# First column piece of v from x times scale, and a new order of the first 140 microseconds

## The chip, the cores and the metric

The kernel runs on one core of one Trainium2 chip. The metric is the device time of that core in microseconds (us), the median of three runs. Five engines matter here: TensorE (PE) for products, VectorE (DVE), ScalarE (ACT), GpSimd (POOL) and SyncE (SP), whose queue issues most of the loads. "Weight load" (PEld) is PE's load of the stationary operand.

## The reference, cut to what matters

One step of a two-layer encoder over 1024 prompt rows and 32 sample rows, with D = 1024. Each layer is a mixer and a feed-forward part, each with an RMS norm before and after it and with a conditioning (shift, scale, gate) that comes from a condition vector.

```
mod = silu(c) @ w_ada[i] + b_ada[i]
sh1, sc1, gt1, sh2, sc2, gt2 = split(mod, 6)
h = rmsnorm(x, g_norm[i, 0]) * (1 + sc1) + sh1
# layer 0: spatial gating
z = gelu(h @ w_in)            # 1024 -> 4096
u, v = split(z, 2)            # 2048 each
v = rmsnorm(v, g_v)
mix = (u * (w_s v + b_s)) @ w_out
x = x + gt1 * rmsnorm(mix, g_norm[i, 1])
# then a feed-forward part of width 4096 with squared ReLU; layer 1 has a pooling mixer
```

With r the root of a row, h = r * x * scale + shift, where scale is g_norm * (1 + sc1) and belongs to a feature, r to a row. So h @ w is r * ((x * scale) @ w) + shift @ w.

## The kernel before

The rows are kept transposed, features on the 128 partitions, in three tiles (`TILES`, L27): two of 384 prompt rows and one of 256 prompt rows with the 32 sample rows. In blocks of 128 rows these are blocks 0 to 2, 3 to 5, and 6, 7 and 8 (the sample rows). Weights and the modulated rows are each split into a high and a low part ("wh", "wl"; "hh", "hl"), and a product is three matmuls: wh with hh, wl with hh, wh with hl. ACT makes wh by a copy (L422), DVE makes wl by a subtraction.

Before anything else stands the v half of the first product. It is made in four column pieces of 512; a piece p of a block b, here (p, b), is 24 matmuls of 128x512 (16 for block 8), into one PSUM place. `v_mm` (L910) issues them, `v_end` (L933) reads the place out: gelu, a square that accumulates, and a store.

To get there the kernel loads x blocks, turns them by TensorE transposes (`x_turn`; copies out by DVE at L586 or ACT at L588), sums squares on ACT (`x_squares`, L565), computes the roots (`spread`, L715: ACT's Sqrt, a reciprocal and a Newton step on DVE), spreads them over the partitions with a diagonal and a product with ones ("pb"), and `apply` (L853) makes mt = x * scale * r on DVE, hh = mt + shift on ACT, hl on DVE. `first_norm(t)` (L887) does this for tile t; its generators are called h0, h1 and h2.

The conditioning is a product with a matrix of 1024 x 6144. A slice is 256 of its columns, two loads of 512 KB. Slices 0 to 3 are the first shift, 4 to 7 the first scale; these are made on PE (`do_ada_pe`, L472: 16 small matmuls, a DVE transpose, a fold "adat"). All later slices are made on DVE (`do_ada`, L500: eight steps "aa" of 128x256 per load, then a transpose and a reduction per slice).

All loads stand in one list, `stream`, and `issue` (L395) issues them in that order on SP, as far as buffers are free: three raw places (`RAW_SLOTS`) for weights and slices that are dropped after use, and 16 places (`W_SLOTS`) for split weights and early raws.

The order around the change is set in two ways. From the first load up to the products of piece 0 a list of calls under `tc.manual_schedule` (L991 to L1047) fixes each engine's order. Everything behind it, including the slices 8 and up, is placed by a planner, which may put an instruction of later code between those of the fixed list. `early_mm` (L961) issues the products of piece 0 for blocks 0 to 4 pair by pair of k, as the modulated rows come; block 5 follows, then `v_order` (L1073): (1,0) to (1,5), then blocks 6 to 8 of pieces 0 and 1, then pieces 2 and 3.

Of the kernel before, what the change touches and what calls it, by code (L numbers as in the profile page):

```python
# [15 lines left out]
P = 128  # L16
# [18 lines left out]
def tile_stream_encoder_step(  # L35
# [144 lines left out]
    def load_vectors(i, part):  # L180
        at = sum(k for _, k in rows[i][: part.start])
        for ap, k in rows[i][part]:
            nc.scalar.dma_start(vec_rows[i][at : at + k, :P], ap)
            at += k
# [6 lines left out]
    def turn_conditions():  # L191
        raw = vec_rows[2]
        nc.vector.memset(csil32, 0.0)
        act(out=raw[0:16, P : 2 * P], in_=raw[0:16, :P], func=AF.Silu)

        act(out=raw[0:16, 2 * P : 2 * P + 1], in_=epsT[0:16, :], func=AF.Sqrt)
# [5 lines left out]
    def turn_vectors():  # L202
        for raw, v in zip(vec_rows, vecs):
            n = v.shape[1]
            pt = ps_ms("rowT")
            nc.tensor.transpose(pt[:, :n], raw[:n, :P], ident[:n, :n])
            nc.vector.tensor_copy(v, pt[:, :n])
# [131 lines left out]
    for b in range(3):  # L339
        add_x(b)  # L340
    for q in range(4):
        for j in (8 + 2 * q, 9 + 2 * q, 2 * q, 2 * q + 1):
            add_ada(0, j)
        add_w(*v_item(0, q))
        if q == 0:
            for b in range(3, 6):
                add_x(b)
# [30 lines left out]
    state = {"issued": 0, "next": 0, "raw": 0, "used": 0, "folds": 0}  # L378
    deferred = []

    def in_raw(k):
# [5 lines left out]
    x_rows = [  # L387
        room("h", t, f"x_rows{t}")
        .rearrange("p k n -> p (k n)")[:, : ncol[t] // P * D]
        .rearrange("p (b k n) -> p b k n", k=KB, n=P)  # L390
        for t in range(NT)
    ]
    junk = room("l", NT - 1, "xsq")

    def issue():  # L395
        while state["issued"] < len(stream):
            k = state["issued"]
            kind, key, ap, shape = stream[k]
            if in_raw(k):
                if state["raw"] == RAW_SLOTS:  # L400
                    return
                state["raw"] += 1
                r = t_raw(f"raw{k}")
            elif kind == "x":
                r = x_rows[key // 3][:, key % 3] if key < 8 else junk[:, :, P : 2 * P]
            else:
                r = work.tile([P, 1024], F32, tag="W", bufs=W_SLOTS, name=f"raw{k}")
            if kind == "x":
                nr = P if key < 8 else DEC
                i = (nc.scalar if key == 2 else nc.sync).dma_start(  # L410
                    r[:nr], ap.rearrange("t (k n) -> t k n", n=P)
                )
            else:
                i = nc.sync.dma_start(r.rearrange("p (a b) -> p a b", a=shape[0]), ap)
            raws[k] = r
            loads[key] = i.ins
            state["issued"] += 1

    def do_w(key, r):
        wh = work.tile([P, 1024], F32R, tag="W", bufs=W_SLOTS, name="wh_" + "_".join(map(str, key)))  # L420
        wl = work.tile([P, 1024], F32R, tag="W", bufs=W_SLOTS, name="wl_" + "_".join(map(str, key)))
        act(out=wh, in_=r, func=AF.Copy)  # L422
        witem[key] = (wh, wl)
        if key == ("v", 0, 0):
            late_lo.append(lambda: tt(out=wl, in0=r, in1=wh.bitcast(F32), op=ALU.subtract))
        else:
            tt(out=wl, in0=r, in1=wh.bitcast(F32), op=ALU.subtract)
# [135 lines left out]
    def x_squares(b, r):  # L563
# [8 lines left out]
    def x_turn(b, r):  # L572
# [3 lines left out]
        for half in range(2):  # L576
# [8 lines left out]
            if half == 0 or t == 0:  # L585
# [5 lines left out]
    x_turns = deque()  # L591

    def do_x(b, r):
        x_squares(b, r)
        if b < 3:
            x_turn(b, r)
        else:
            x_turns.append(lambda: x_turn(b, r))
# [10 lines left out]
    def stream_step():  # L609
# [18 lines left out]
        if in_raw(k):  # L628
# [85 lines left out]

    def spread(t, ss, tag, out, dg):  # L715
# [5 lines left out]
        ts(ms[:, :nb], ss[:, :nb], 1.0 / D, EPS, op0=ALU.mult, op1=ALU.add)  # L721
        act(out=r0[:, :nb], in_=ms[:, :nb], func=AF.Sqrt)
        nc.vector.reciprocal(out=r0[:, :nb], in_=r0[:, :nb])
        tt(out=q[:, :nb], in0=r0[:, :nb], in1=r0[:, :nb], op=ALU.mult)
        stt(out=q[:, :nb], in0=q[:, :nb], scalar=-0.5, in1=ms[:, :nb], op0=ALU.mult, op1=ALU.mult)
        stt(out=r0[:, :nb], in0=q[:, :nb], scalar=1.5, in1=r0[:, :nb], op0=ALU.add, op1=ALU.mult)
        yield False
        pb = ps_ms(f"pb_{tag}")
        for b, (c0, w) in enumerate(blk):
            act(out=dg[:w, c0 : c0 + w], in_=ident[:w, :w], func=AF.Copy, scale=r0[:w, b : b + 1])  # L730
        for b, (c0, w) in enumerate(blk):
            mm(pb[:, c0 : c0 + w], ones[:w, :], dg[:w, c0 : c0 + w], start=True, stop=True)
        out.append(pb)
# [119 lines left out]
    def apply(t, l, cf, sh, r, keep=False):  # L853
        hh[t] = room("h", t, f"hh{l}_{cf}_{t}", F32R)
        hl[t] = room("l", t, f"hl{l}_{cf}_{t}", F32R)
# [40 lines left out]

    def products(ps, n, terms):
# [8 lines left out]

    ssqv = small.tile([P, 9, 4], F32, name="ssqv")
# [25 lines left out]
    def v_end(ps, p, b):  # L933
        m = P if b < 8 else DEC
        vt = t_x(f"vt{p}_{b}", [P, 512])
        z = ps
        if b == 8:
# [21 lines left out]
    h0, h1, h2 = (first_norm(t) for t in range(NT))  # L959

    def early_mm(bs, q):  # L961

        wh, wl = witem[("v", 0, q)]
        for second in (False, True):
            for b in bs:
                t, c0 = b // 3, b % 3 * P
                tick(0.46 if second else 0.92)
                for k in range(2):
                    kb = 2 * q + k
                    a_h, a_l = hh[t][:, kb, c0 : c0 + P], hl[t][:, kb, c0 : c0 + P]  # L970
                    w = slice(k * 512, k * 512 + 512)
                    for a in (a_h,) if second else (a_h, a_l):
                        mm(
                            early_ps[b],
                            a,
                            (wl if second else wh)[:, w],
                            start=kb == 0 and a is a_h and not second,
                            stop=kb == KB - 1 and second,
                        )
# [5 lines left out]
    def conditions(q):  # L985

        stream_to("ada", (0, 4 + q, 1))
        stream_to("ada", (0, q, 1))
        pe_folds.pop(0)()

    with tc.manual_schedule():  # L991
        load_vectors(2, slice(0, 2))
        issue()
        load_vectors(2, slice(2, 4))
        load_vectors(0, slice(0, 1))
        load_vectors(1, slice(0, 1))
        turn_conditions()
        stream_to("x", 1)
        turn_vectors()
        stream_to("x", 2)  # L1000
        next(h0)
        conditions(0)
        statistics(h0)
        stream_to("w", ("v", 0, 0))
        pe_folds.pop(0)()
        for q in range(4):
            next(h0)
            if q == 0:
                late_lo.pop()()
            early_mm((0, 1, 2), q)  # L1010
            if q == 0:
                stream_to("x", 5)
                next(h1)
                x_turns.popleft()()
                x_turns.popleft()()
                next(h1)
                x_turns.popleft()()
                statistics(h1)
            next(h1)
            if q < 3:  # L1020
                conditions(q + 1)
                stream_to("w", ("v", 0, q + 1))
                early_mm((3,), q)
                pe_folds.pop(0)()
                early_mm((4,), q)
                if q == 2:
                    stream_to("x", 6)
            else:
                early_mm((3, 4), q)
        stream_to("x", 8)  # L1030
        while x_turns:
            x_turns.popleft()()
        next(h2)
        ps = ps_ms("pv0_5")
        v_mm(ps, 0, 5, range(KB))
        next(h2)
        early_end((0,))
        stream_to("w", ("v", 1, 1))
        early_end((1, 2))
        stream_to("w", ("v", 1, 2))  # L1040
        early_end((3,))
        stream_to("w", ("v", 1, 3))
        early_end((4,))
        statistics(h2)
        v_end(ps, 0, 5)
# [13 lines left out]
    rv = small.tile([P, 9], F32, name="rv")  # L1059
    rms = small.tile([P, 9, 2], F32, name="rms")  # L1060

# [11 lines left out]
    v_order = [(1, b) for b in range(6)] + [(p, b) for p in range(2) for b in range(6, 9)]  # L1073
# [68 lines left out]
    def sgu_group(g):  # L1142
        wt = sgu.tile([P, P], F32, tag="wt", bufs=2, name=f"wt{g}")
        nc.sync.dma_start(wt, sgu_w_s[0, g])
        bb = sgu.tile([P, P], F32, tag="bs", bufs=2, name=f"bs{g}")
        nc.scalar.dma_start(bb, sgu_b_s[0, g].partition_broadcast(P))
# [527 lines left out]
```

## Time and profile before

| | |
|---|---|
| median of 3 runs | 2175.01 us (2173.2 to 2175.78) |
| the profiled execution | 2173.74 us, its span 2171.7 us |
| PE busy | 2145.5 us, 99% of the span |
| DVE busy | 1431.8 us, 66% |
| ACT busy | 971.3 us, 45% |
| first product of v | at 19.77 us |
| (1,0) begins | at 77.47 us |
| (2,0) begins | at 142.45 us |

In the rows of the profile a line number is that of the kernel before; L79 is the helper that issues nearly every DVE instruction, so such rows are told apart by their tiles. A timeline row gives start, duration, engine, line, operation, output and inputs, shape, and in brackets the idle time ahead of it with what ended it. A grouped row gives the number of instructions, the busy time, the mean of one in ns, and the idle time ahead of them. Instructions of an engine overlap by some tens of ns, so the distance from one start to the next is a better price than the duration. A windows row gives for each engine busy time and instructions, then the granted clock of PE, the DMA engines' share and GB/s.

### The profile page before, as it was taken

The page shows a single profiled execution, that of the slowest core. Times are in us where ns is not written, and L with a number is a line of the kernel's source. Part 1 is how long each engine was busy: PE and PEld are TensorE (multiplying, and loading weights), DVE is VectorE, ACT ScalarE, POOL GpSimd, SP SyncE. Part 2 cuts the span into 40 slices and gives each one's busy share as a digit, 9 for nine tenths or more (in the row PEclk, how much of TensorE's full clock was granted, in tenths as well). Part 3 has the DMA queues.
Part 4 walks back from the last instruction along what each step waited for, and adds up shares of the span by engine and source line. Part 5 has one row for each costly group of instructions (what it writes and reads, how often), then busy time and mean ns, then how long its engine had stood idle before and what let it go on. Part 6 is the DMA issues. An engine that isn't in the chain of part 4 may idle for free.

```text
span 2171.7 us, 33210 instructions
## 1 busy us (share of the span) xinstructions
PE 2145.5 (99%) x13214; PEld 2078.1 (96%) x13214; DVE 1431.8 (66%) x2499; ACT 971.3 (45%) x1643; POOL 13.3 (1%) x30
## 2 busy tenths in 40 slices
PE   7999999999999999999999999999999999999998
PEld 5778899999999999999999999999999999999997
DVE  5688647566879548496747879869675554523377
ACT  4633422234447552323445566666555542313354
POOL 0000000000000000000000000000000000000001
PEclk9999999999999999999999999999999999999999
DMA  8386534343437454243645466565455552302255
GB/s 300 119 269 193 173 93 139 90 148 109 147 96 233 132 155 143 87 140 110 196 129 161 141 189 182 171 191 158 141 161 158 157 155 68 98 20 78 69 139 125
DMA packets 383262, 312.95 MB, mean 144 GB/s; under 512 B 39458, under 2 KB 346346, under 8 KB 383108
## 3 DMA queue, kind: packets, MB, share of 16 engines
q1 hardware_dynamic: 380452, 308.64, 46.8%
q8 instruction: 103, 1.69, 0.3%
q10 hardware_dynamic: 2144, 1.41, 0.2%
q0 software_dynamic: 512, 0.79, 0.1%
q14 instruction: 51, 0.42, 0.1%
HBM read 278.95 MB, written 31.84 MB: 143 GB/s over the span
## 4 chain that ended last, share of the span: by engine, by line
PE 93%; DVE 3%; DMA 2%; ACT 1%; issue 1%; ACTq 0%; DVEq 0%; SPq 0%
PE pg L902 11%; PE pg L903 11%; PE pg L904 11%; PE pf L902 11%; PE pf L904 11%; PE pf L903 11%; PE po L902 3%; PE po L903 3%; PE po L904 3%; PE pu L902 3%; PE pu L904 3%; PE pu L903 3%; PE pv L929 2%; PE pv L930 2%; PE pv L931 2%; PE pp L1532 1%
## 5 line engine op out<-in xcount | busy, mean ns | idle before, releaser
L902 PE MATMUL pg<-fh,wh_dn 128*128 128x384 f32 (+1 forms) x1536 | 495.8, 323 | 0.0
L902 PE MATMUL pf<-hh,wh_up 128*128 128x384 f32 (+1 forms) x1536 | 494.4, 322 | 0.0
L903 PE MATMUL pf<-hl,wh_up 128*128 128x384 f32 (+1 forms) x1536 | 493.1, 321 | 0.0
L904 PE MATMUL pf<-hh,wl_up 128*128 128x384 f32 (+1 forms) x1536 | 492.9, 321 | 0.2 <-DVE wl_up L79 0.2
L903 PE MATMUL pg<-fl,wh_dn 128*128 128x384 f32 (+1 forms) x1536 | 492.6, 321 | 0.4 <-DVE fl L79 0.4
L904 PE MATMUL pg<-fh,wl_dn 128*128 128x384 f32 (+1 forms) x1536 | 492.5, 321 | 0.0
L79 DVE TENSOR_TENSOR wl_up<-raw,wh_up 128x1024 fp32r<-128x1024 f32 x152 | 185.9, 1224 | 165.4 <-ACT wh_up L422 165.4
L902 PEld LDWEIGHTS pg<-fh,wh_dn 128*128 128x128 f32 x1536 | 288.3, 188 | 1.5 <-ACT fh L1121 0.6
L903 PEld LDWEIGHTS pg<-fl,wh_dn 128*128 128x128 f32 x1536 | 288.3, 188 | 1.5 <-DVE fl L79 0.7
L904 PEld LDWEIGHTS pf<-hh,wl_up 128*128 128x128 f32 x1536 | 288.6, 188 | 0.5 <-DVE wl_up L79 0.5
L903 PEld LDWEIGHTS pf<-hl,wh_up 128*128 128x128 f32 x1536 | 288.3, 188 | 0.4
L902 PEld LDWEIGHTS pf<-hh,wh_up 128*128 128x128 f32 x1536 | 288.2, 188 | 0.4
L904 PEld LDWEIGHTS pg<-fh,wl_dn 128*128 128x128 f32 x1536 | 288.3, 188 | 0.0
L422 ACT ACTIVATE wh_up<-raw 128x1024 fp32r<-128x1024 f32 x152 | 161.2, 1060 | 279.9 <-PE pf L903 213.6
L79 DVE TENSOR_TENSOR acc<-acc,pg 128x384 f32<-128x384 f32 (+1 forms) x336 | 174.2, 519 | 146.3 <-PE pg L904 145.7
L422 ACT ACTIVATE wh_dn<-raw 128x1024 fp32r<-128x1024 f32 x152 | 160.8, 1059 | 202.9 <-PE pg L903 170.6
L79 DVE TENSOR_TENSOR wl_dn<-raw,wh_dn 128x1024 fp32r<-128x1024 f32 x152 | 186.0, 1224 | 82.4 <-ACT wh_dn L422 82.2
L79 DVE SCALAR_TENSOR_TENSOR aa<-raw,csil,aa 128x512 f32<-128x512 f32 (+1 forms) x364 | 203.5, 623 | 8.0 <-DMA raw<-in_w_ada_dram 7.9
L1295 ACT ACTIVATE r<-pf 128x384 f32<-128x384 f32 (+1 forms) x192 | 86.6, 451 | 201.9 <-PE pf L904 199.2
L79 DVE TENSOR_TENSOR fl<-r,fh 128x384 fp32r<-128x384 f32 (+1 forms) x192 | 100.3, 523 | 85.4 <-ACT fh L1121 84.3
L902 PE MATMUL pu<-hh,wh_u 128*128 128x384 f32 (+1 forms) x384 | 125.8, 328 | 0.0
L902 PE MATMUL po<-ush,wh_o 128*128 128x384 f32 (+1 forms) x384 | 123.5, 322 | 0.0
(263 smaller groups left out, 2927.2 us busy)
## 6 DMA issues: line engine op xcount, KB each, us to landing
raw<-in_ffn_w_up_dram SPq DMA_DIRECT2D x152, 512.0 KB, 3.9
raw<-in_ffn_w_down_dram SPq DMA_DIRECT2D x152, 512.0 KB, 3.5
raw<-in_w_ada_dram SPq DMA_DIRECT2D x96, 512.0 KB, 4.3
raw<-in_sgu_w_in_dram SPq DMA_DIRECT2D x40, 512.0 KB, 4.4
xd<-acc SPq DMA_DIRECT2D x8, 1536.0 KB, 7.8
raw<-in_sgu_w_out_dram SPq DMA_DIRECT2D x24, 512.0 KB, 4.0
xo_r<-xd SPq DMA_DIRECT2D x32, 384.0 KB, 3.4
vd<-vt SPq DMA_DIRECT2D x32, 256.0 KB, 4.5
```

The lines of the kernel that those rows point to most:

```text
L79: return op(out, *args, **kw)
L422: act(out=wh, in_=r, func=AF.Copy)
L902: mm(ps[:, :n], wh, rh, start=i == 0, stop=False)
L903: mm(ps[:, :n], wh, rl, start=False, stop=False)
L904: mm(ps[:, :n], wl, rh, start=False, stop=i == last)
L929: mm(ps[:m, :], a_h, wh[:, o : o + 512], start=k == 0, stop=False)
L930: mm(ps[:m, :], a_h, wl[:, o : o + 512], start=False, stop=False)
L931: mm(ps[:m, :], a_l, wh[:, o : o + 512], start=False, stop=k == KB - 1)
L1295: act(out=r[:, :n], in_=ps[:, :n], func=AF.Relu)
L1532: mm(ps[:, :n], wg[:, k, e * P : (e + 1) * P], A(t, 2 * g + k), start=k == 0, stop=k == 1)
```

## The change

It does these things together.

- The list of loads begins with x0, the two loads of slice 4, and the first weights; the other x blocks and slices 5 to 7 follow between the weights of piece 0, and slices 0 to 3 (the shift) come behind them. Early raws may take up to half of the 16 places.
- Piece 0 of tiles 0 and 1 is made from x * scale ("hx" by ACT, "lx" by DVE, `scaled`), without r and without shift, so that only scale is needed to begin. Blocks 0 to 2 (`front`) come first, then 3 to 5 (`rear`).
- r comes in at the read-out: for blocks 0 to 2 by an ACT copy with scale rv (`early_read`), which frees the PSUM place early, for blocks 3 to 5 in `v_end`.
- The shift's part is a row shift @ w, made by 16 matmuls of 128x512 with two stationary columns (`shift_products`), spread by a product with ones (`spread_shift`) and added in `v_end` (six DVE operations of 512 columns).
- The modulated tiles 0 and 1, which the later pieces need, are still made (`full`): tile 0's between the products of `rear`, tile 1's while piece 1 is being made. (1,0) to (1,2) move into the fixed list, and the splits of piece 1's weights stand between the last products of `rear` and (1,0).
- 16 throwaway products of 128x512 (`warm`) are issued before the condition rows are turned and around the first slice.
- The root uses Abs_reciprocal_sqrt in place of Sqrt and a reciprocal; a dummy Silu loads its table early; some small loads move to POOL's queue or to another place of ACT's, and the loads of sgu_w_s and sgu_b_s wait for the last weights of piece 2.

```
-        for j in (8 + 2 * q, 9 + 2 * q, 2 * q, 2 * q + 1):
+        if q == 0:
+            add_x(0)
+        for j in (8 + 2 * q, 9 + 2 * q):
             add_ada(0, j)
         add_w(*v_item(0, q))
+        for b in ((1, 2), (), (3, 4, 5), ())[q]:
+            add_x(b)
+    for j in range(8):
+        add_ada(0, j)
...
+    def scaled(t, ks, c0, w):
...
+        for k in ks:
+            act(out=hh[t][:, k, c0 : c0 + w], in_=A(t, k, c0, w), func=AF.Copy,
+                scale=coef[:, 0, 0, 0, k : k + 1])
+        for k in ks:
+            stt(out=hl[t][:, k, c0 : c0 + w], in0=A(t, k, c0, w),
+                scalar=coef[:, 0, 0, 0, k : k + 1],
+                in1=hh[t][:, k, c0 : c0 + w].bitcast(F32), op0=ALU.mult, op1=ALU.subtract)
...
+    def full(t):
+        cp = t_c(f"r_h0_{t}")
+        pb = diagonals(t, rv[:, 3 * t : 3 * t + 3], [(c * P, P) for c in range(3)], cp, f"h0_{t}")
+        act(out=cp[:, : ncol[t]], in_=pb[:, : ncol[t]], func=AF.Copy)
+        yield False
+        yield from apply(t, 0, 0, 0, cp, keep=True)
...
+        if p == 0 and b < 3:
+            tt(out=vt, in0=vt, in1=bias[0], op=ALU.add)
+        elif p == 0 and b < 6:
+            stt(out=vt, in0=ps, scalar=rv[:, b : b + 1], in1=bias[0], op0=ALU.mult, op1=ALU.add)
...
     with tc.manual_schedule():
...
+        warm(10)
         turn_conditions()
+        stream_to("x", 0)
+        x_turn(0)
...
+        slice_(4)
+        warm(3)
+        x_squares(0)
+        fold()
+        warm(3)
+        weights(0, 0)
+        scaled(0, (0, 1), 0, P)
+        early_mm((0,), (0, 1), False)
...
+        stream_to("x", 8)
+        weights(1, 0)
+        slice_(3)
+        early_mm(rear, (6, 7), False)
+        fold()
+        next(f0)
+        row = shift_products()
+        weights(1, 1)
+        early_mm(rear, (6, 7), True)
+        next(f0)
+        spread_shift(row)
+        weights(1, 2)
+        roots_of(1)
+        turn_vector(2)
+        x_turn(6)
+        weights(1, 3)
+        ps = ps_dn("pv1_0")
+        v_mm(ps, 1, 0, range(KB))
+        for b in front:
+            early_end((b,))
+        x_turn(7)
+        x_turn(8)
+        f1 = full(1)
...
-    v_order = [(1, b) for b in range(6)] + [(p, b) for p in range(2) for b in range(6, 9)]
+    v_order = [(1, b) for b in range(3, 6)] + [(p, b) for p in range(2) for b in range(6, 9)]
```

More of the change, by code (lines that the diff above doesn't have):

```diff
@@ L377, in tile_stream_encoder_step @@
     loads = {}
-    state = {"issued": 0, "next": 0, "raw": 0, "used": 0, "folds": 0}
+    state = {"issued": 0, "next": 0, "raw": 0, "used": 0, "folds": 0, "early": 0}
     deferred = []
@@ L627, in stream_step @@
         state["next"] += 1
-        if in_raw(k):
+        if k < first_ada and (kind == "ada" or key == 5):
+            state["early"] -= 1
+        if in_raw(k) and not (kind == "w" and key[:2] == ("v", 0)):
             state["raw"] -= 1
@@ L720, in spread @@
         ms, r0, q = t_st(f"ms_{tag}"), t_st(f"r0_{tag}"), t_st(f"q_{tag}")
[L721 to L726, printed above, removed]
-        yield False
[L728 to L733, printed above, removed]
+        roots(r0[:, :nb], ms[:, :nb], q[:, :nb], ss[:, :nb])
+        yield False
+        out.append(diagonals(t, r0, blk, dg, tag))
         yield False
@@ L904, in products @@
             mm(ps[:, :n], wl, rh, start=False, stop=i == last)
+    rv = small.tile([P, 9], F32, name="rv")
+    rms = small.tile([P, 9, 2], F32, name="rms")
+    bias = []
+    early_vt = {}
     ssqv = small.tile([P, 9, 4], F32, name="ssqv")
@@ L983, in early_end, with slice_, fold, weights @@
             v_end(early_ps[b], 0, b)
-    def conditions(q):
-        stream_to("ada", (0, 4 + q, 1))
-        stream_to("ada", (0, q, 1))
+    def slice_(sl):
+        stream_to("ada", (0, sl, 1))
+    def fold():
         pe_folds.pop(0)()
+    def weights(p, q):
+        stream_to("w", ("v", p, q))
+    def shift_products():
+        x = shift[:, 0, 0, :, 0]
+        parts_of_shift = small.tile([P, KB, 2], F32R, name="parts_of_shift")
+        act(out=parts_of_shift[:, :, 0], in_=x, func=AF.Copy)
+        tt(
+            out=parts_of_shift[:, :, 1],
+            in0=x,
+            in1=parts_of_shift[:, :, 0].bitcast(F32),
+            op=ALU.subtract,
+        )
+        prow = ps_dn("prow")
+        for k in range(KB):
+            for w in witem[("v", 0, k // 2)]:
+                mm(
+                    prow[0:2, :],
+                    parts_of_shift[:, k, :],
+                    w[:, k % 2 * 512 : k % 2 * 512 + 512],
+                    start=k == 0 and w is witem[("v", 0, 0)][0],
+                    stop=k == KB - 1 and w is witem[("v", 0, 3)][1],
+                )
+        row = work.tile([P, 512], F32, tag="aa", bufs=2, name="shift_row")
+        act(out=row[0:2, :], in_=prow[0:2, :], func=AF.Copy)
+        return row, prow
@@ new lines, in spread_shift, with early_read, roots_of @@
+    def spread_shift(got):
+        row, prow = got
+        pbias = ps_dn("pbias")
+        mm(pbias, ones[0:2, :], row[0:2, :], start=True, stop=True)
+        bias.append(work.tile([P, 512], F32, tag="aa", bufs=2, name="shift_rows"))
+        act(out=bias[0], in_=pbias, func=AF.Copy)
+        bias.append(prow)
+    def early_read(b):
+        vt = early_vt[b] = t_x(f"vt0_{b}", [P, 512])
+        act(out=vt, in_=early_ps[b], func=AF.Copy, scale=rv[:, b : b + 1])
+    def roots_of(t):
+        c = slice(3 * t, 3 * t + 3)
+        roots(rv[:, c], rms[:, c, 0], rms[:, c, 1], ssx[:, c])
@@ L991, in tile_stream_encoder_step, with warm @@
+    front, rear = (0, 1, 2), (3, 4, 5)
+    fresh = onesr.unsqueeze(1).broadcast_to([P, 4, P])
+    def warm(n):
+        for _ in range(n):
+            mm(early_ps[4].rearrange("p (a b) -> p a b", a=4), onesr, fresh, start=True, stop=True)
     with tc.manual_schedule():
-        load_vectors(2, slice(0, 2))
+        load_vectors(nc.scalar, 2, slice(0, 2))
         issue()
-        load_vectors(2, slice(2, 4))
-        load_vectors(0, slice(0, 1))
-        load_vectors(1, slice(0, 1))
+        load_vectors(nc.scalar, 1, slice(0, 1))
+        load_vectors(nc.scalar, 0, slice(0, 1))
+        act(out=vec_rows[2][64:80, P : P + 1], in_=epsT[64:80, :], func=AF.Silu)
+        warm(10)
@@ new lines, in tile_stream_encoder_step @@
+        weights(0, 3)
+        scaled(0, (6, 7), 0, 3 * P)
+        x_squares(3)
+        early_mm(front, (6, 7), False)
+        late_lo.pop()()
+        scaled(1, (0, 1), 0, 3 * P)
+        x_squares(4)
+        x_squares(5)
+        early_mm(front, (6, 7), True)
+        roots_of(0)
+        slice_(0)
+        early_ps.append(ps_ms("pv0_5"))
+        early_mm(rear, (0, 1), False)
+        fold()
+        f0 = full(0)
+        next(f0)
+        for b in front:
+            early_read(b)
+        early_mm(rear, (0, 1), True)
```

267 lines of the change are left out of this document (163 added, 104 removed).

## The prediction

> **What bounds the kernel now.** I read the page from the top: busy times, the slices, the chain of work that ended last.
>
> ```profile
> span 2171.7 us, 33210 instructions
> PE 2145.5 (99%) x13214; PEld 2078.1 (96%) x13214; DVE 1431.8 (66%) x2499; ACT 971.3 (45%) x1643; POOL 13.3 (1%) x30
> PE   7999999999999999999999999999999999999998
> PE 93%; DVE 3%; DMA 2%; ACT 1%; issue 1%; ACTq 0%; DVEq 0%; SPq 0%
> ```
>
> PE is busy 99% of the span and carries 93% of the chain. Only the first slice stands below 9, and the change lies in the first three. So I went on to the windows of the start, cut where block 0 of the third column piece, here (2,0), begins: from there on both programs do the same work behind a busy PE. The second answer is DVE's alone.
>
> ```profile
> core 0: us, PE busy (x) PEld busy (x) DVE busy (x) ACT busy (x) POOL busy (x), PEclk, DMA share, GB/s
> 0.00:142.45 142.45, 128.66 (x711) 96.90 (x711) 96.15 (x251) 70.18 (x140) 0.69 (x6) 0.96 0.65 218
> 15.90:19.30 3.40, 1.92 (x34) 1.32 (x30) 1.82 (x6) 2.01 (x5) 0.00 (x0) 1.00 1.03 418
> 19.30:26.10 6.80, 6.33 (x14) 4.75 (x15) 3.27 (x9) 4.47 (x9) 0.00 (x0) 0.50 1.08 384
> 84.86:125.42 40.56, 38.97 (x171) 31.37 (x171) 40.03 (x109) 18.71 (x48) 0.00 (x0) 1.00 0.58 183
> 142.45:160.00 17.55, 17.55 (x79) 14.53 (x78) 11.41 (x28) 5.57 (x12) 0.00 (x0) 1.00 0.92 307
> core 0: us, DVE busy (x), PEclk, DMA share, GB/s
> 0.00:103.50 103.50, 61.56 (x173) 0.95 0.62 211
> 0.00:125.42 125.42, 83.40 (x226) 0.96 0.62 208
> ```
>
> Three readings. PE has no idle time after 142.45 (17.55 of 17.55), so whatever (2,0) gains or loses stays in the total: the whole forecast is when (2,0) begins. DVE has 40.03 us of work in the 40.56 us from 84.86 on, yet PE isn't stopped by it. And the granted clock was 0.50 for 6.8 us as the products of v began.
>
> Why does a full DVE not stop PE? The timeline of that stretch says it.
>
> ```profile
> 77.47 0.51 PE L929 MATMUL pv<-wh_v,hh 128*128 128x512 f32 x1
> 84.01 0.39 PE L931 MATMUL pv<-wh_v,hl 128*128 128x512 f32 x1
> 84.23 0.39 PE L929 MATMUL pv<-wh_v,hh 128*128 128x512 f32 x1
> 101.55 0.65 DVE L79 SCALAR_TENSOR_TENSOR mt<-acc,coef,r_h 128x256 f32<-128x256 f32 x2
> 102.11 0.69 DVE L532 TENSOR_REDUCE sums<-raw 128x16 f32<-128x512 f32 x1
> 103.40 0.23 DVE L1056 CAST hs<-hl 128x128 fp32r<-128x128 f32 x1
> 109.35 0.35 DVE L79 TENSOR_SCALAR aa<-raw,csil 128x256 f32<-128x256 f32 x1
> 116.60 0.35 DVE L79 TENSOR_SCALAR aa<-raw,csil 128x256 f32<-128x256 f32 x1
> 142.45 0.40 PE L929 MATMUL pv<-wh_v,hh 128*128 128x512 f32 x1
> ```
>
> DVE finishes the modulated third tile (h2) with the small cast at 103.40. Slice 9 of the conditioning is then worked off, slice 10 begins at 109.35 and slice 11 at 116.60: 7.25 us of DVE for each slice, and three of the four stand **behind** h2. Piece 1 on PE begins at 77.47; the (0,6) to (0,8) and (1,6) to (1,8) products, which need h2, come after six blocks of 24 products at 84.23 - 84.01 = 0.22 to 0.23 us, thus at about 110. DVE was 7 us early.
>
> **The change: how early v begins.** Before, the first product of v waits for three x blocks, their root and two conditioning slices.
>
> ```profile
> 6.15 0.31 ACT L194 ACTIVATE row<-row 16x128 f32<-16x128 f32 x1
> 6.47 1.28 ACT L196 ACT_TABLE_LOAD   x1
> 6.79 3.68 PE L580 MATMUL xT<-ident,x_rows 128*128 128x128 f32 x16
> 13.40 3.45 PE L477 MATMUL ada<-raw,csil 128*32 128x256 f32 x32
> 15.40 0.45 DVE L489 STREAM_TRANSPOSE adas<-ada 128x256 f32<-128x256 f32 x1
> 17.45 0.17 DVE L79 SCALAR_TENSOR_TENSOR coef<-coef,vec 128x4 f32<-128x4 f32 x1
> 19.77 0.79 PE L973 MATMUL pv<-wh_v,hh 128*128 128x512 f32 x1 [1.85 <-ACT hh L875]
> 22.30 0.63 PE L973 MATMUL pv<-wh_v,hl 128*128 128x512 f32 x1
> 22.73 0.63 PE L973 MATMUL pv<-wh_v,hh 128*128 128x512 f32 x1
> 27.08 2.04 PE L580 MATMUL xT<-ident,x_rows 128*128 128x128 f32 x16
> 45.53 1.93 PE L477 MATMUL ada<-raw,csil 128*32 128x256 f32 x32
> ```
>
> After, it needs x0 (8 transposes, half of 3.68, so 1.8), one slice (half of 3.45: 1.7), its fold, coef and one ACT copy. The dummy Silu takes a table load (1.28) off the ACT path ahead of the condition rows, so PE can start at about 5.8 rather than 6.6: 5.8 + 1.8 + 0.8 (two small transposes) + 1.7 + 1.2 (stream transpose 0.45, fold, coef 0.17 twice, copy) = 11.3. If the throwaway products don't help and a load comes late, 12.5. So the first product comes 7.3 to 8.5 us earlier; I take 8.5.
>
> Does the clock help? The same 128x512 product takes 22.73 - 22.30 = 0.43 us there and 0.23 later; 16 transposes take 3.68 at first and 2.04 at 27.08. The window ahead of the half clock, 15.90 to 19.30, had PE busy 1.92 of 3.40 us, so at most 1.48 us idle, and the next two windows were granted half. The Trainium skill, page "TensorE: Matmul & The Clock Gate", section "HAM oscillation — how this bites in real kernels", gives as the rule that PE should have no idle gaps beyond about 3.4 us, else the clock is halved; this case's trace differs: 1.48 us of idle was enough, and the measurement decides. By the rule the change's front would stay warm throughout.
>
> By the row, any half-busy window of the front goes cold, for 3.4 us at half pace, which is 1.7 us of work lost each time; that price returns below.
>
> **Front and rear.** With blocks 0 to 2: 72 products x 0.228 = 16.4, 40 transposes at 2.04 / 16 = 5.1, three slices at 1.93 / 2 = 2.9: 24.4 us of PE. Each pair of k needs an ACT copy, a DVE split and a weight split just ahead; following the written order of each engine I count 6.5 us of waits (three of 1.1 to 1.2 for the pairs, 1.2 for the first low half, 1.8 for the last pair). The front ends at 42.4. Blocks 3 to 5, without their last six products: 66 x 0.228 = 15.0, four slices 3.9, broadcast and folds 1.3, 2.5 of waits: shift 3 is ready at 65.6. The least, with no wait at all in front and rear, is 56.
>
> **DVE: the term that decides.**
>
> ```profile
> 34.38 1.15 DVE L79 SCALAR_TENSOR_TENSOR hl<-mt,shift,hh 128x384 fp32r<-128x384 f32 x2 [0.16 <-ACT hh L875]
> 76.69 2.36 DVE L79 TENSOR_TENSOR wl_v<-raw,wh_v 128x1024 fp32r<-128x1024 f32 x2 [4.59 <-ACT wh_v L422]
> 128.37 0.67 DVE L79 TENSOR_TENSOR vt<-vt,pv 32x512 f32<-32x512 f32 x1
> L941 ACT ACTIVATE vt<-pv 128x512 f32<-128x512 f32 x16 | 9.4, 591 | 23.0 <-PE pv L931 19.5 <-DMA vd<-vt 3.5
> L586 DVE COPY acc<-xT 128x512 f32<-128x512 f32 x11 | 7.6, 692 | 12.2 <-PE xT L580 12.2
> DVE aa L79 <- DMA raw<-in_w_ada_dram: 3.2, 2, 2.6
> ```
>
> The change adds to DVE 16 splits "lx" of 128x384 (1.15 / 2 = 0.575 each: 9.2) and six bias adds of 512 columns (0.67 each: 4.0), and takes off two copies of 0.69 and three reciprocals: +11.3. Worse is the order. In the changed program's order on DVE, all of slices 8 to 11 stand ahead of the last pieces of h2, woven between the read-outs and the full modulation of tile 1, which is moved there. Before h2 is done DVE must therefore do what it did up to 125.42 in the kernel before, 83.40, plus 11.3: about 95 us, where before it had done 61.56 by 103.50 and stood idle 103.50 - 61.56 = 41.9.
>
> By steps, behind shift 3 (65.6): three weight splits 3 x 1.2 = 3.6; the last 8 splits and products of tile 0's modulation 4.6; all 16 of tile 1's 9.2; bias 4.0; slices 4 x 7.25 = 29.0; three x copies 2.1, small rows 1.6; h2 16 pairs x (102.11 - 101.55 = 0.56) = 9.0, casts 0.6. Sum 63.7. Added waits: 5.4, while the second weight split waits for ACT, where the copy of the shift row stands ahead of it and itself waits for PE's 16 shift products (PE reaches them only when tile 0's pair is through DVE and ACT, at 68.5, then 16 x 0.228 = 3.65); and 2.6, as the row of waits shows for a slice that waits for its load, DVE standing still with everything queued behind. h2 ends at 65.6 + 63.7 + 8.0 = 137.3.
>
> On PE meanwhile: the tile-2 transpose waits for a PSUM place that a copy on DVE behind four slice steps frees (75.1 to 82.1), piece 1's block 0 ends at 88.2, the transposes of x7 and x8 and the broadcast wait again (88.9 to 93.3), then blocks 1 and 2 (11 us), 3 to 5 (16.4 and some 6 of waits for tile 1's pieces): 127.4. These waits cost nothing more, because PE then stands for h2 anyway.
>
> Behind h2's last split PE has 6 products of (0,6) and (0,7), some 14 of (0,8), and 64 of (1,6) to (1,8): 84 x 0.228 = 19.2. (2,0) begins at 137.3 + 19.2 = 156.5, against 142.45: **+14.0 us**.
>
> The rest in one place: 16 shift products and their broadcast (3.65 + 1.0 on PE) lie in the path to 137.3 only through the 5.4 above. Early reads, copies and squares on ACT cost nothing: ACT was busy 70.18 of 142.45; without that cover each read would cost the 0.59 of the like copy at L941. Rows put on POOL's queue and the later loads of sgu have nothing waiting in this stretch; at worst a load of 2.6 late, at best nothing, taken as 0. Table loads (1.28 each, two more before h2's root) lie in ACT's idle time. The half clock ahead of h2 is covered too; in the tail, one cold window of 3.4 us would add 1.7.
>
> **Bounds.** If DVE stands idle just 8.5 less than before (the start gained), h2 ends at 95 + 33.4 = 128.4 and (2,0) comes at 147.6: +5. With no idle behind shift 3 and no PE wait ahead of it, 56.2 + 63.7 + 19.2 = 139.1: -3.4. With the cold window of the tail, a second late load and four cold windows in front and rear that push shift 3 itself back, 14.0 + 1.7 + 2.6 + 4 x 1.7 = +25.
>
> **Rivals.**
> *The early start is kept* (faster). If DVE's idle time falls from 41.9 to under 28 (142.45 - 19.2 - 95), its queue isn't late and PE's own sum decides: 8.5 gained at the start, 4.7 lost to shift products, and up to 5 of the waits between 60 and 87 gone: -4 to -9, 2165 to 2170. For it: 12.2 of before's 41.9 are waits for transposes, as the row of x copies shows, and the new order spreads those; and the slice steps may fall into time in which DVE would wait anyway. Against it: they stand ahead in the order, and 29 us of them don't fit into gaps of 1 or 2 us. Chance 0.12.
> *Gain and DVE debt cancel* (within 0.2%, 4.3 us, about what a measurement of this kernel can tell from no change): h2 ends at 119 to 128, idle 24 to 33. Chance 0.08.
> *The clock and the loads bite too*: half-busy windows such as 15.90 to 19.30 recur in front and rear and push shift 3 itself back, 1.7 us for each cold window; four of them and a late load, over the 14: 2197 to 2203. Chance 0.18. By the rule of the Trainium skill's page named above, only the two PE waits of 7.0 and 4.4 us would halve the clock, and both are hidden.
> *The throwaway products and the early slice don't do what they are there for*, since loads land late: start at 12.5 or more, 1 to 3 us on the sum, inside the forecast's own range, and counted there.
>
> **How the numbers follow.** The profiled execution took 2173.74, the median of the runs is 2175.01, 1.27 above. Forecast: 2175.0 + 14.0 = 2189, slower, with chance 0.62 for its own range 2180 to 2197, that is +5 to +22. The third rival adds 0.18: slower 0.80, faster 0.12, same 0.08. To leave out no more than 2 in 10, the range goes from 2173, beside the lower bound of 56.2 + 63.7 + 19.2, to 2201, near the upper bound.
>
> **What would show it.** Right: the first product of v near 11 to 12; shift 3 near 66; DVE busy without a break from about 73 on, with slice steps between the pieces of tile 1; h2's last cast near 137; PE idle for h2 between 127 and 137; (2,0) near 156; the same pace after it. Wrong: h2's last cast before 123, or PE without idle time from 95 on, or a shift in time behind (2,0), which would mean that the rest of the kernel is not the same.

## The result, and the profile after

The changed kernel takes 2194.39 us (median of 4 runs, 2191.8 to 2196.12); the kernel before, run beside it, 2174.11 (2172.04 to 2175.78). The ratio on record is 1.0103, with a 95% interval of 1.009 to 1.0115 (the two medians give 1.0093, inside it): slower by 20 us. The forecast was 2189, slower, range 2173 to 2201. The size came out near. The reason given for it did not hold, and the experiments below are mostly about that.

The page of the changed kernel, the lines that were read before:

```profile
span 2189.8 us, 33339 instructions
PE 2158.6 (99%) x13248; PEld 2079.2 (95%) x13248; DVE 1442.1 (66%) x2519; ACT 986.2 (45%) x1672; POOL 14.3 (1%) x32
PE   8899999999999999999999999999999999999998
```

The span is 18.1 us longer than before's 2171.7. The first slice of PE, which stood at 7, is now 8, and the second, which stood at 9, is 8 as well. The timeline of the changed kernel gives the marks of the prediction one by one: the first product of v, the last shift, the first shift product, the transposes of x6, (1,0), (0,6), h2's last cast, and (2,0).

```profile
11.33 0.50 PE L1036 MATMUL pv<-wh_v,hx 128*128 128x512 f32 x1
70.58 0.16 DVE L79 TENSOR_TENSOR shift<-adat,vec 128x4 f32<-128x4 f32 x1 [1.11 <-PE adat L480]
73.24 0.40 PE L1071 MATMUL prow<-wh_v,parts_of_shift 128*2 128x512 f32 x1 [2.72 <-DVE parts_of_shift L79]
87.66 1.11 PE L603 MATMUL xT<-ident,x_rows 128*128 128x128 f32 x4 [5.78 <-DVE vec L207]
88.43 0.78 PE L987 MATMUL pv<-wh_v,hx 128*128 128x512 f32 x1
129.91 0.39 PE L987 MATMUL pv<-wh_v,hh 128*128 128x512 f32 x1
141.33 0.22 DVE L1241 CAST hs<-hl 128x128 fp32r<-128x128 f32 x1
160.11 0.39 PE L987 MATMUL pv<-wh_v,hx 128*128 128x512 f32 x1
```

(2,0) begins at 160.11 instead of 142.45, which is 17.7 of the 18.1 us. Behind it the two traces run alike (2029.7 and 2029.3 us to the end of the span). Of the 17.7, 11.0 are lost by (1,0), which was at 77.47, though v begins 8.4 us earlier; another 6.7 between (1,0) and (2,0). The windows, cut at these marks, show how:

```profile
core 0: us, PE busy (x) PEld busy (x) DVE busy (x) ACT busy (x) POOL busy (x), PEclk, DMA share, GB/s
11.33:46.55 35.22, 30.09 (x184) 19.68 (x185) 16.57 (x33) 16.96 (x30) 0.00 (x0) 0.95 0.93 337
46.55:73.24 26.69, 23.09 (x170) 14.58 (x169) 13.57 (x30) 10.72 (x21) 0.00 (x0) 1.00 0.26 87
73.24:88.43 15.19, 9.41 (x34) 4.31 (x34) 7.19 (x17) 4.32 (x7) 0.00 (x0) 0.77 0.19 58
99.65:130.00 30.35, 29.00 (x129) 23.22 (x129) 30.35 (x76) 23.33 (x50) 0.00 (x0) 1.00 0.51 168
130.00:160.11 30.11, 30.06 (x130) 21.89 (x129) 20.33 (x53) 16.23 (x35) 0.00 (x0) 1.00 0.62 205
```

Two rows matter. In 73.24 to 88.43 PE is busy 9.41 of 15.19 us at a granted clock of 0.77, and no other engine is busy for half of it either (DVE 7.19, ACT 4.32): three engines wait for each other. The first rows of that chain are ACT's copy of the shift row, which waits for PE's 16 shift products, and DVE's next weight split, which waits for the ACT copy behind it:

```profile
78.71 0.59 ACT L1079 ACTIVATE shift_row<-prow 2x512 f32<-2x512 f32 x1 [6.15 <-PE prow L1071]
80.28 1.22 DVE L79 TENSOR_TENSOR wl_v<-raw,wh_v 128x1024 fp32r<-128x1024 f32 x1 [7.09 <-ACT wh_v L437]
```

Behind that split DVE comes to the copy for which the transposes of x6 wait (5.78 us, at 87.66 above). In 130.00 to 160.11, where the prediction has PE standing for h2, PE is busy 30.06 of 30.11. DVE was full from 99.65 to 130.00 (30.35 of 30.35), as forecast, and PE was still busy 29.00 us of it. The cover for h2 is thin, though: DVE's last split of h2 begins at 140.63, and PE's last products with the low part of h2 in (0,6) and (0,7) begin at 141.37 and 142.06.

So there were two theories to tell apart. That of the prediction: DVE's queue, with slices 8 to 11 ahead of h2, sets (2,0). Its rival: PE's own waits ahead of 100, in the chain of the shift and at the transposes of x6, are the delay, and the late h2 is covered by products that PE has anyway. In the lists below every version is an edit of the changed kernel, unless it says "before".

### The profile page after: what moved, and what is told of

It is laid out like the page before. It is cut to its first block, busy times and chain, and to the rows that moved or that the text cites. A ratio compares the mean times of both kernels' runs of the same rounds, so it can differ in the third digit from the quotient of the medians.

```text
span 2189.8 us, 33339 instructions
## 1 busy us (share of the span) xinstructions
PE 2158.6 (99%) x13248; PEld 2079.2 (95%) x13248; DVE 1442.1 (66%) x2519; ACT 986.2 (45%) x1672; POOL 14.3 (1%) x32
## 4 chain that ended last, share of the span: by engine, by line
PE 92%; DVE 3%; DMA 2%; ACT 1%; SPq 1%; issue 1%; DVEq 0%; ACTq 0%
PE pg L956 11%; PE pg L957 11%; PE pg L958 11%; PE pf L956 11%; PE pf L958 11%; PE pf L957 11%; PE pu L956 3%; PE pu L958 3%; PE pu L957 3%; PE po L957 3%; PE po L956 3%; PE po L958 3%; PE pv L987 2%; PE pv L989 2%; PE pv L988 2%; PE psp L1396 1%
## 5 line engine op out<-in xcount | busy, mean ns | idle before, releaser
L957 PE MATMUL po<-usl,wh_o 128*128 128x384 f32 (+1 forms) x384 | 123.3, 321 | 0.0
```

The source lines that it names most:

```text
L957: mm(ps[:, :n], wh, rl, start=False, stop=False)
```

## Experiments

| version | median us | over before beside it, us | ratio to before, 95% interval | (1,0) at | (2,0) at |
|---|---|---|---|---|---|
| before (first profile) | 2174.11 | | 1 | 77.47 | 142.45 |
| changed | 2194.39 | 20.3 | 1.0103 (1.009 to 1.0115) | 88.43 | 160.11 |
| slices behind h2 | 2196.16 | 23.6 | 1.011 (1.0093 to 1.0127) | 86.60 | 157.15 |
| vector turned later | 2190.98 | 18.4 | 1.0085 (1.0069 to 1.0101) | 83.83 | 159.75 |
| shift chain earlier | 2190.10 | 17.5 | 1.0083 (1.0062 to 1.0104) | 85.73 | 158.34 |
| both chains | 2186.81 | 14.2 | 1.0067 (1.005 to 1.0084) | 80.56 | 156.98 |
| both, splits spread | 2181.67 | 10.8 | 1.0053 (1.0038 to 1.0068) | 77.36 | 151.75 |
| the same, more mended | 2178.50 | 8.2 | 1.0043 (1.0027 to 1.0059) | 76.90 | 147.64 |
| more mended, 2 of 16 shift products | 2177.58 | 5.9 | 1.0029 (1.0017 to 1.0041) | 77.59 | 147.71 |
| changed, 2 of 16 shift products | 2190.73 | 19.9 | 1.0089 (1.0072 to 1.0105) | 89.35 | 162.02 |
| changed, no throwaway products | 2194.39 | 23.6 | 1.0112 (1.0097 to 1.0127) | 91.91 | 163.30 |
| before, with throwaway products | 2169.32 | -1.5 | 0.9993 (0.9984 to 1.0003) | | 137.40 |
| the same, sgu loads later | 2168.68 | -1.6 | 0.9994 (0.9985 to 1.0003) | | 138.03 |

The kernel before was run again beside each group of versions, and its median was between 2170.26 and 2174.11. So medians of different groups can't be compared as they stand; the third column takes off the median of before from the same group. The last two columns are from one profiled execution each, the median from several; the start of a trace moves from one execution to the next (the first shift product stood at 73.24, 73.67 and 75.18 in three versions with the same order up to there, and at 78.97 in one that began with a late load).

**Slices 8 to 11 behind h2.** The theory of the prediction, taken at its word:

```
-    some_ada(8)
     for p in range(2, 4):
         w_vpiece(p)
-        some_ada(8)
+        some_ada(8 if p == 2 else 16)
```

> The changed kernel with slices 8 to 11 of the conditioning streamed behind the weights of piece 2, so that on DVE they stand behind h2 instead of ahead of it. Theory of the prediction (DVE's queue decides when (2,0) begins): h2's last cast goes from 141.4 to 110 to 115, and (2,0) comes 9 us or more earlier than its 160.1, a time of 2185 or less. Rival (PE's own waits between 72 and 100 are the delay, and the late h2 is covered by products that PE has anyway): h2 is as early, but (2,0) moves by 4 us at most, a time of 2190 to 2194.

Measured: 2196.16, no gain, and h2 was not as early as either theory had it. Its DVE timeline shows why, from tile 1's third pair to h2's last cast:

```profile
113.43 1.15 DVE L79 SCALAR_TENSOR_TENSOR lx<-mt,shift,hx 128x384 fp32r<-128x384 f32 x2 [5.55 <-ACT hx L899]
122.85 0.65 DVE L79 SCALAR_TENSOR_TENSOR mt<-acc,coef,r_h 128x256 f32<-128x256 f32 x2 [4.46 <-ACT r_h L917]
136.78 0.22 DVE L1240 CAST hs<-hl 128x128 fp32r<-128x128 f32 x1
```

With 29 us of slice work taken off DVE ahead of it, h2 ends only 4.5 us earlier (136.78 for 141.33), and DVE stands still in the gaps that the slices had filled: 5.55 us for ACT's part of tile 1 and 4.46 for the root's broadcast. DVE alone from the last shift to the end of h2, in the changed kernel and then here (us, DVE busy, granted clock of PE, DMA share, GB/s):

```profile
70.58:141.55 70.97, 61.55 (x155) 0.93 0.41 133
71.01:137.00 65.99, 34.23 (x83) 0.95 0.23 80
```

DVE's work falls by 27 us and the stretch by 5. The written order ties h2 to ACT's work on the tiles before it, not to DVE's load. (2,0) moves by 3 us, as the rival said, though with an h2 only 4.5 us earlier. And the time is not better, because the loads that were put later are late elsewhere: between 250 and 300 PE idles 3.05 us and its granted clock falls to 0.93, where the changed kernel had 49.97 of 50 and 1.00; the longest of the waits, 2.52 us, is for the copy of a weight that ACT gets from its load at 254.09, after 3.70 us of waiting. So here a gain at (2,0) did not stay in the total, against the prediction's first reading.

```profile
250.00:300.00 50.00, 46.95 (x270) 44.86 (x269) 42.29 (x85) 20.92 (x33) 0.31 (x1) 0.93 0.66 202
```

The prediction's theory falls here: neither the place of the slices nor DVE's load sets the end of h2 or (2,0).

**The two chains on PE, each alone and together.** In the changed kernel the transposes of x6 wait for a PSUM place: block 5's product has taken one of the pool's three for the whole stretch, the first half of x6 takes another, and the turn of the third vector tile holds the last until DVE copies it out; that copy stands behind the root of tile 1. The first edit moves that turn behind block 5's read-out:

```
-        turn_vector(2)
         x_turn(6)
 ...
         early_end((5,))
+        turn_vector(2)
```

The second makes the shift's two parts ahead of tile 0's next pair and lets the last six products of blocks 3 to 5 run before the shift products:

```
         fold()
+        parts = shift_parts()
+        early_mm(rear, (6, 7), True)
         next(f0)
-        row = shift_products()
+        row = shift_products(parts)
         weights(1, 1)
-        early_mm(rear, (6, 7), True)
```

> The changed kernel with the turn of the third vector tile (pool_scale and sgu_g_v) moved behind block 5's read-out, so that the transposes of x6 no longer wait for the PSUM place that it holds. Theory of the prediction: nothing, since PE stands for h2 later anyway; 2193 to 2195. Rival: the 5.8 us of PE idle at 81.9 and the half clock behind it go, 5.8 + 1.7 = 7.5 us at most, 2187 to 2190.

> The changed kernel with the two parts of the shift made ahead of tile 0's next pair on ACT and DVE, and the last six products of blocks 3 to 5 put ahead of the 16 shift products. Theory of the prediction: nothing on the total. Rival: PE's 2.7 us of idle ahead of the shift products go and the half-clock window of 74.6 to 78.1 with them (1.7), so 3 to 4.4 us less, 2190 to 2191.

> The edits of the two runs before together (third vector tile later, shift chain earlier); slices 8 to 11 still ahead of h2. If DVE's queue decides: 2192 to 2194. If PE's waits decide and add up: 10.5 to 12 us less, 2182 to 2184. If both are close (PE 11 us early, then standing for h2): something between, with PE idle at 120 to 140.

Measured: 2190.98, 2190.10, and 2186.81 together. Against before beside them, each alone is 2 to 3 us better than the changed kernel (4 by the ratios), with intervals that overlap its own; together 6.1 us (7.8 by the ratios), with intervals apart. The prediction's theory expected nothing of any. Windows of PE alone (us, PE busy, granted clock, DMA share, GB/s), first of the changed kernel:

```profile
76.00:92.00 16.00, 10.22 (x34) 0.72 0.27 82
65.00:80.00 15.00, 12.13 (x63) 0.89 0.13 35
```

the same stretch with the vector turned later:

```profile
76.00:92.00 16.00, 13.82 (x52) 0.89 0.21 66
```

and with the shift chain earlier:

```profile
65.00:80.00 15.00, 12.72 (x70) 1.00 0.12 36
```

PE's busy time in 76 to 92 rises from 10.22 to 13.82 with the vector turned later, and the granted clock from 0.72 to 0.89. With the shift chain earlier PE's wait ahead of the shift products goes, and the clock of 65 to 80 is 1.00 instead of 0.89; that the edit brought the clock is not shown, since the run with the slices behind h2 had 1.00 there with the same wait of 2.72 us. Together the two edits came out between the times that the two theories expected. The gain was less than the 10.5 to 12 us that the rival expected: with the shift chain earlier alone the wait at x6 grew to 6.42 us, and what was mended uncovered 0.76 and 1.09 us of waits for the next weight splits, at 87.89 and 91.23 in the trace of the vector turned later. In the trace of both chains the granted clock was 0.54 from 93.0 to 100.5. That PE then stood for h2 is not seen: it was busy 19.75 of 20 us from 120 to 140.

**Weight splits and the squares of x5.** Next come those waits, and one that the prediction had missed: in the changed kernel the fourth low half of piece 0 waits for a place in memory.

```profile
43.68 1.23 DVE L79 TENSOR_TENSOR wl_v<-raw,wh_v 128x1024 fp32r<-128x1024 f32 x1 [3.62 <-ACT xsq L587]
```

The row says that a weight split waits 3.62 us for a square of x rows, with which it shares no data. What they share is memory: x5 sits in one of the 16 places of the split weights, and the place comes free only when ACT has squared it, after x3 and x4. The edit squares x5 first, x3 and x4 behind it, and puts piece 1's second split ahead of the shift products.

```
         scaled(0, (6, 7), 0, 3 * P)
-        x_squares(3)
+        x_squares(5)
 ...
         slice_(3)
+        weights(1, 1)
```

> The version with both chains mended, further with the squares of x block 5 taken ahead of those of 3 (the fourth low half waits for its buffer until they are done) and the second weight split of piece 1 ahead of the shift products. If PE's waits decide: 1 us and a half-clock window of 1.7 at 40 to 45, and 1 to 2 us of the waits for weight splits at 84 to 92: 2182 to 2184. If the queue of DVE decides: as the version with both chains, 2186 to 2187.

Measured: 2181.67, on the rival's side (10.8 us over before, from 14.2; the intervals of the two versions overlap). The split's wait falls from 3.62 to 0.40 us, so the place of x5 was its cause, and the last shift comes 58.1 us behind the first product of v, where the changed kernel has 59.3. The next edit takes the rest of the waits that its trace showed:

```
         fold()
+        warm(8)                  # ahead of the fourth weights; warm(5) ahead of the third
         weights(0, 3)
 ...
         next(f0)
+        weights(1, 2)
         row = shift_products(parts)
+        f1 = full(1)             # tile 1's broadcast, from behind (1,0)
+        next(f1)
```

with tile 1's roots made beside tile 0's.

> The version with the second split ahead and both chains mended, further with the third split of piece 1 ahead of the shift products, tile 1's roots and broadcast ahead of (1,0) instead of behind it, and 5 and 8 throwaway products in the two waits of the front (1.19 and 1.96 us). If PE's waits and half-clock windows are the delay: 0.85 and 1.45 us of waits and two half-clock windows of 1.7 go, about 5 us, 2176 to 2178, and what is left over the kernel before is the added products (4.8) and the short covers of the front. If not: 2181 to 2182.

Measured: 2178.50, just above the 2176 to 2178 expected. Waits alone, with no work taken out and some throwaway products added, are thus worth 12 us of the 20 (20.3 over before, then 8.2; by the ratios on record 13). In all these versions (2,0) begins 18.2 to 18.6 us behind the end of h2's last cast, as in the changed kernel: h2 became early as PE did, with no work taken off DVE.

**How many of the products that the change adds count?** With 2 of the 16 shift products, in the changed kernel and in the most mended one:

> The changed kernel with 2 of the 16 shift products, so that the shift's part of the output holds only the first of the 8 features blocks; the chain of copies, broadcast and adds stays. If PE's own sum decides: 14 products less, 3.2 us at full clock and up to 4.9 as half of them ran at half clock: 2189 to 2191. If DVE or ACT decide: 2194.

> The most mended version (third split ahead, tile 1's broadcast ahead, throwaway products in the front) with 2 of the 16 shift products, so that the shift's part of the output holds only the first of the 8 feature blocks. If what that version still lacks on the kernel before is PE's added work: 14 products of 0.23, 3.2 us less, 2175 to 2176. If the copies and the broadcast of the shift row are on the path instead, which stay: 2178 to 2179.

Neither run settles it. In the changed kernel the median is 3.7 us less (2190.73, runs from 2186.9 to 2193.3), but only 0.4 less over before beside it; its (2,0) was no earlier, but that trace began with a late load, the first product at 14.32. In the mended one the median is 0.9 less and, over before beside it, 2.4 (ratio 1.0029 for 1.0043, with intervals that overlap). Its trace has (2,0) at 147.71 against 147.64, so there nothing was gained, and it shows what takes the products' place; the timeline's row of PE behind the shift products, with 2 of them:

```profile
72.39 1.65 PE L739 MATMUL pb_h<-r_h,ones 128*128 128x128 f32 x6 [2.10 <-ACT r_h L737]
```

and with all 16:

```profile
73.99 1.07 PE L739 MATMUL pb_h<-r_h,ones 128*128 128x128 f32 x6 [0.97 <-ACT r_h L737]
```

The window of PE around it, again with 2:

```profile
67.00:77.00 10.00, 7.90 (x34) 0.77 0.50 157
```

and with all 16:

```profile
67.00:77.00 10.00, 9.03 (x50) 1.00 0.50 157
```

3.2 us of products come out, PE's idle time in the ten us rises from 0.97 to 2.10, and the clock of the stretch falls from 1.00 to 0.77. So in this trace it is ACT's diagonal that is late, and the gap that the products had filled lets the clock fall.

**The throwaway products.** Out of the changed kernel, and into the kernel before without the rest of the change:

> The changed kernel without the 16 throwaway products. If the clock of the start sets the first product of v: it comes 1.5 to 2 us later (12.8 to 13.3 instead of 11.33), the first products run at half clock, and the total is 2 to 4 us longer, 2196 to 2198. If loads set it: no change, 2194.

> The kernel before with throwaway products alone: 10 at first, 3 behind the vector turns, 6 in the 1.85 us of idle ahead of the first product of v, 6 in the idle ahead of slice 5's fold. If PE's clock in the first 40 us is on the path: the half-clock windows of 19.3 to 26.1 and 36.4 to 39.8 go, worth 3.4 and 1.7, and the first transposes run faster: 5 to 7 us less than before, 2165 to 2168. If later waits for loads and weight splits take it back: 2171 to 2174.

```
+        warm(10)
         turn_conditions()
 ...
         turn_vectors()
+        warm(3)
 ...
         pe_folds.pop(0)()
+        warm(6)
         for q in range(4):
 ...
         stream_to("ada", (0, q, 1))
+        if q == 1:
+            warm(6)
```

Taking them out of the changed kernel moves the first product from 11.33 to 12.38. The medians are the same (2194.39 both), but over before beside it the version without them is 3.3 us slower, with intervals that overlap, and its trace has (2,0) 3 us later. Whether they help the changed kernel is left open. In the kernel before the stretches that ran at half clock no longer do:

```profile
15.90:19.30 3.40, 3.13 (x33) 1.00 1.03 414
19.30:26.10 6.80, 6.36 (x34) 1.00 1.08 384
36.40:39.80 3.40, 3.25 (x14) 1.00 1.06 356
```

The granted clock was 0.50 in the last two; now it is 1.00, and (2,0) comes at 137.40, 5.05 us earlier. The time is in neither of the two expected ranges: the median of 10 runs is 2169.32, against 2170.84 for before in the same runs: 1.5 us, with an interval that holds no change. Before's first profile (2173.74) is longer than the median of its later runs, so some of the 5 us may be that one trace. One more try, with the sgu loads held back:

> The kernel before with the throwaway products (as in the run with those alone) and the loads of sgu_w_s and sgu_b_s held back until the last weights of piece 2. The throwaway products alone moved (2,0) by 5 us in the trace and the time by 1.5, within the error. If the loads of the start set what is left (the DMA engines' share is 1.0 between 11 and 34): 256 KB less at 390 GB/s, 0.7 us, 2168 to 2169. If not: 2169 to 2171.

2168.68 against 2170.26, again 1.6 us and an interval from 0.9985 to 1.0003. Both versions of before are the fastest here, and neither is proven faster than before.

## Why the prediction was right, and where it was wrong

- *The start*: 11.3 forecast, 11.33 measured; 8.4 us gained.
- *Front and rear*: the front was to end at 42.4 and ended at 46.55, shift 3 was to come at 65.6 and came at 70.58. In the front PE's waits came to 5.1 us, fewer than the 6.5 counted; PE's work was 30.1 us where the sum has 24.4. The sum leaves out three folds of 0.25, it prices every product at 0.228 though the first of a group takes 0.34 to 0.52 from start to start, and about seven products ran at half clock, 0.43 each. The wait list was made from data and queues; it left out memory that is handed on, the place of x5 (3.62 us of DVE's wait, then 0.95 of PE's). In two traces in which the clock stayed full there (vector turned later, both chains), PE waited 2.5 us for that split and went on no earlier, so the split set the pace and not the half clock. The most mended version has shift 3 at 67.80.
- *The shift chain*: PE was to idle from 65.6 to 68.5, 2.9 us; measured 2.72.
- *The x6 transposes*: 7.0 us forecast, 5.78 measured, followed by 3.4 us at half clock. The wait was foreseen and priced at nothing; moving it away alone brought some 2 us (18.4 for 20.3 over before, not resolved), and together with the shift chain 6.1.
- *DVE's bill*: from shift 3 to h2's end 71.7 us forecast, 141.33 + 0.22 - 70.58 = 71.0 measured, of it 61.55 busy where the bill has 63.7. As a count of DVE's work the bill was right; that it also gave the end of h2 was luck. Without the 29 us of slices it would be 42.7, and the run with the slices behind h2 took 66.0.
- *What decides*: here the prediction's mechanism failed. "These waits cost nothing more, because PE then stands for h2 anyway" doesn't hold: PE's own sum had been worked out to 127.4 for the end of (1,5), and from there 128 products at 0.228 make 156.6, a tenth from where the h2 path ended (156.5). Two paths of the same length, and only one was called the bound; that the size came out near whichever of them decides is luck too. Of the 128 products 84 were charged behind h2's end; the other 44 (10.0 us) were left out, and they fill just the time from 127.4 to 137.3 in which PE was to stand. The trace has PE busy 30.06 of 30.11 there, and taking PE's earlier waits away brought 12 of the 20 us. The run with the slices behind h2 shows that the other path isn't DVE's queue either.
- *The total*: +14.0 forecast for (2,0), +17.7 measured; the difference is about that of the front. The rival of cold windows was right in kind: half-clock windows at 40, 75 and 88, and 0.77 over 73.24 to 88.43. Its sum takes each of them in full, and the one at 40 cost nothing, as said above.
- *The Trainium skill's rule* (page "TensorE: Matmul & The Clock Gate", section "HAM oscillation — how this bites in real kernels") that gaps beyond 3.4 us halve the clock would have had only the 5.78 us wait do so. The trace went to half behind waits of 1.96 and 2.72 too, as the row of before had it; but not every such wait did it, as the last section shows.

What stays open: the 8 us that the most mended version still has over before. In its trace (1,0) begins at 76.90, as early as before's 77.47; the 5.2 us of its (2,0) lie behind that, where the transposes of x7 and x8, their waits, and a wait of 1.79 us for ACT's read-out with a half-clock window now are. From (1,0) to (2,0) PE is busy 68.03 us there and idle 2.71, before 63.39 and 1.59. No run took these out. What the added shift products cost is not resolved, and the smaller parts of the change (the root's function, the moved small loads) were not taken back one by one. Nor was it tried to make piece 0 of all six blocks together from x * scale, which would give the front's waits more products to hide behind.

## What to carry to other kernels

When two paths to the same instruction come out within a few us, neither may be called the bound and the waits on the other priced at nothing; take each away by itself. A wait with no shared data (a weight split on a square, a transpose on a vector copy) was both times here a buffer being handed on: find whose place it takes, and reorder the holder. An earlier start is worth what the narrower work behind it can hide: here each step had 18 products of cover instead of 30, and some of the short waits were paid twice, once in time and once in clock.

## What the runs showed of the hardware

The granted clock fell to half behind short waits of PE: behind 1.48 us of idle time in a 3.4 us window (before, at 15.9; the whole wait there is 1.85) and behind 1.96 (changed, at 37). But the length of a wait alone doesn't tell. PE's windows from the end of a wait on, with the granted clock as the number behind the bracket: the changed kernel and the one with the slices behind h2 after the same wait of 2.72 us, then the most mended version with all shift products and with 2 of them after 1.79 and 1.80 us.

```profile
73.24:80.00 6.76, 6.76 (x23) 0.75 0.00 0
73.67:80.00 6.33, 6.33 (x25) 1.00 0.00 0
109.68:116.00 6.32, 6.32 (x22) 0.73 0.76 250
110.94:117.00 6.06, 6.06 (x28) 1.00 0.81 263
```

In each pair the first lost some 1.7 us and the second nothing. What makes the difference was not tested. In the kernel before, throwaway products that kept PE busy over 90% of the three stretches shown kept the clock full there. A full queue on DVE with fillers, 30.35 of 30.35 us busy, was not a bound: with the fillers gone h2 ended 4.5 us earlier, not 29.
